# Table sets of ScalarE asked for by name in a linear attention, and silu of two gate units one product later

## The chip, the cores and the metric

The kernel runs on one core of one Trainium2 chip. The metric is the device time of one execution in microseconds (us). The engines are TensorE (PE; its weight loads are shown apart as PEld), VectorE (DVE), ScalarE (ACT), GpSimd (POOL) and SyncE (SP, which here issues most DMAs). ACT evaluates functions from a table that holds one set of functions at a time. An ACT_TABLE_LOAD brings in another set.

## The reference

One layer of a streaming encoder, 512 tokens of width 2048, all in float32. The part that matters here is the input projection and the gated linear attention behind it:

```python
proj = h @ w_in[i]
q_a, k_a, v_a, q_g, k_g, v_g, r_g, gate_lr = split_cols(proj, IN_SPLITS)
gate_logit = gate_lr @ w_gla_gate_up[i] + b_gla_gate[i]
log_a = jax.nn.log_sigmoid(gate_logit) / GLA_GATE_TAU      # 4 heads of 128 keys
o_g = gated_linear_attention(q_g, k_g, v_g, log_a)         # exp(b), exp(-b), exp(b_last - b), b a sum over a chunk
o_g = rms_norm(o_g, gla_norm_w[i])
y_g = o_g * jax.nn.silu(r_g)
x = x + jnp.concatenate([y_a, y_g], axis=-1) @ w_out[i]
```

Before it stands an RMSNorm, beside it a banded softmax attention (16 heads), and after it a gated MLP with a causal convolution and GELU, an embedding gate with a sigmoid, and a last RMSNorm.

## The kernel before, in words

Every large product is cut into units of 256 output rows by 512 tokens. A unit is computed by seven half-size products (P1, P2, P6, P5, P7, P3, P4 in this order) instead of eight. Each float32 operand is split into a high and a low part of float32r, so a product is three runs of 8 matmuls: high weights with high input, high weights with low input, low weights with high input. A product takes 2.72 us on PE.

One list, `steps`, holds all products of the program in order, and the loop at line 1350 emits one step after the other. What a step emits stays in program order on each engine: ACT, DVE and PE instructions go through the wrapper at line 64, which is why nearly every row of the profile bears L64. For a step i the loop emits in this order: the items of the agenda with key 0 (DMAs), the high half of the weights of step i+2 (`prep_high`, ACT, rows wsplit<-l and wsplit<-s), the items with key 1, the low half (`prep_low`, DVE, rows wsplit<-l,wsplit), the matmuls, the items with keys over 1, and last the eviction of the product's PSUM bank (`collect`). A product whose quarter of the output is new is copied out by ACT (rows u<-accA, u<-accC); another is added by DVE. The next product on the same bank waits for that. Split weights live in a ring of three pages, outputs of units in a ring of two, u0 and u1, in this part. So a unit's first copy waits until the unit before last has been stored.

The first stage, `linear` (line 1068), has ten units in this order: head 0, two value units, head 1, two value units, head 2, gate unit 0, gate unit 1, head 3. The stage after it, `front`, starts with the softmax heads. A head unit gives the keys and queries of a linear-attention head (`gla_head`). Its own ACT work is spread over the steps around it:

- two steps into the unit, `softplus` and `logs`: Abs (row e<-pz), Exp and Ln (rows e<-e), which give log_sigmoid together with DVE's lf, then DVE's running sum cs and the differences dd
- `powers` and `falls`, two steps later: four Exp (rows eb, en, dd, dec)
- during the units behind it, `root` and `rooted`: Identity (nwa), Ln and Exp (both rows rg) and Square (nwt) of the head's mean square; DVE finishes (rows nwt, rg) and scales the output (row og)

A gate unit (`after_gates`) multiplies its output by the norm of the input on DVE (u<-u,rb), applies Silu on ACT (u<-u), multiplies by the head's output on DVE (u<-u,on) and stores the operands of the output projection through SP (rows mix_R<-u, mix_N<-tp and so on).

The kernel does not say which table set ACT is to hold. When the program is built, an ACT_TABLE_LOAD is put ahead of each function that the set in force lacks, and the set is chosen per function: one for Exp, one for Ln, one for Silu.

Of the kernel before, what the change touches and what calls it, by code (L numbers as in the profile page):

```python
# [11 lines left out]
AF = mybir.ActivationFunctionType  # L12
# [31 lines left out]
def encoder_block(ctx: ExitStack, tc: tile.TileContext, A, out):  # L44
    nc = tc.nc
# [24 lines left out]
    vec, act, ten = InOrder(nc.vector), InOrder(nc.scalar), InOrder(nc.tensor)  # L70
# [13 lines left out]
    rb = cp.tile([P, T], F32, name="rb")  # L84
    rtok = cp.tile([P, TT], F32, name="rtok")
    cw = cp.tile([P, 2 * FB, 4], F32, name="cw")

    counts = {}

# [173 lines left out]
    def store_pair(xd, k, a, b, t=None):  # L263

        t = (page("x", "tp") if t is None else t).rearrange("p (o t) -> p o t", o=4)
        a0, a1, b0, b1 = a[:, 0:256], a[:, 256:512], b[:, 0:256], b[:, 256:512]
        ops = dict(R11=a0, R21=b0, R22=b1, N1=t[:, 0, :], T3=t[:, 1, :], N2=t[:, 2, :], T4=t[:, 3, :])

        def store(*names):
            for op in names if xd else ():  # L270
                store_operand(xd, op, k, ops[op])

        store("R11", "R21", "R22")
        vec.tensor_tensor(ops["N1"], a0, a1, ALU.subtract)
        store("N1")
        vec.tensor_tensor(ops["T3"], b1, a1, ALU.subtract)
        store("T3")
        vec.scalar_tensor_tensor(ops["N2"], ops["N1"], -1.0, b1, ALU.mult, ALU.subtract)
        store("N2")
        vec.scalar_tensor_tensor(ops["T4"], ops["N2"], -1.0, b0, ALU.mult, ALU.subtract)  # L280
        store("T4")
        return ops
# [573 lines left out]
    def after_gates(unit):  # L856
        g, M = unit.u - 8, unit.M

        def times():
            vec.tensor_tensor(unit.o, unit.o, M["on"], ALU.mult)  # L860

        def pair():
            ops = store_pair(mixd if g < 3 else None, 3 + g, unit.o[:, 0, :], unit.o[:, 1, :])
            if g == 3:
                tails[1] = ops

        return [(0, 1, lambda: vec.tensor_tensor(unit.o, unit.o, rb2, ALU.mult)),
                (0, 2, lambda: act.activation(unit.o, unit.o, AF.Silu))] + (
                    [(4, 1, times), (5, 1, pair)] if g < 2 else [(1, 1, times), (1, 3, pair)] if g == 2 else
                    [(0, 3, times), (0, 4, pair)])  # L870

# [2 lines left out]
    def gt(name, tag, cols=T):  # L874
        return gla["pool"].tile([P, cols], F32, tag=tag, name=name)
# [17 lines left out]
    def gla_head(unit):  # L893
# [14 lines left out]
            act.activation(e, e, AF.Exp, scale=-1.0)  # L908

        def logs():  # L910
            act.activation(M["e"], M["e"], AF.Ln, bias=1.0)

        def least():
# [9 lines left out]
                              ALU.subtract)  # L923

        def powers():
            for n, k in (("eb", 1.0), ("en", -1.0)):
                M[n] = gt(n, n)
                act.activation(M[n], M["cs"], AF.Exp, scale=k / TAU)
# [11 lines left out]
        def gates_begin():  # L940
            i = base[unit]
            for t, k, f in ((0, 0, load_v), (0, 6, logits), (1, 2, softplus), (1, 3, least), (2, 2, logs), (3, 1, sums),
                            (4, 1, powers), (4, 3, falls), (6, 1, decays)):
                agenda[i + t].append((k, f))
# [405 lines left out]
    for i, (unit, prod) in enumerate(steps[:-4]):  # L1350
# [19 lines left out]
        if i - len(steps) in EARLY:  # L1370
            p, op, g = EARLY[i - len(steps)]
# [160 lines left out]
```

## Time and profile before

| what | value |
|---|---|
| median of 3 runs (lowest to highest) | 2251.08 us (2249.51 to 2252.3) |
| the profiled execution | 2249.89 us |
| its span on the core | 2248.2 us |
| PE busy | 2196.9 us, 98% of the span |
| DVE busy | 1926.6 us, 86% |
| ACT busy | 1351.5 us, 60% |
| ACT_TABLE_LOAD | 31 in the ordered part and one at the start, 1283 ns each |
| mean granted clock of PE | 0.995 |

A busy PE is not a PE at its peak: ends of matmuls are modelled. What can be read well is where PE waits. A row of the timeline has start, duration, engine, line, operation, output <- input, shapes and count. In brackets stands the idle time of the engine before it and whose work ended that time.

### The profile page before, as it was taken

The numbers are of one execution on the slowest core, as the hardware profiler recorded it, in microseconds if no ns is written. First come the engines' busy times: TensorE is split into PE (matmuls) and PEld (weight loads), VectorE is DVE, ScalarE is ACT, GpSimd is POOL, SyncE is SP. The second block draws the span as 40 slices with busy tenths as digits, with TensorE's granted clock in tenths as the row PEclk, the third lists the DMA queues.
The fourth block names the chain that finished last, engine by engine and source line by source line (L and its number), as shares of the span: only waits on it lengthen the run. The fifth ranks groups of instructions, "written<-read, shape, count | busy, mean of one in ns | idle before, by whom it ended". The sixth has DMA issues, their size and how long they took to land. (4 is left out here: it accounts for less than half of the span.)

```text
span 2248.2 us, 46272 instructions
## 1 busy us (share of the span) xinstructions
PE 2196.9 (98%) x18588; PEld 2145.7 (95%) x18588; DVE 1926.6 (86%) x2636; ACT 1351.5 (60%) x2010; POOL 158.7 (7%) x196
## 2 busy tenths in 40 slices
PE   9999999999999999999999999999999999999995
PEld 8899989999889999999999999999999999999995
DVE  8476777999879888999988898889898887999996
ACT  9455565777665665555555555555564554667655
POOL 0000000000000100000000000010000100000000
PEclk9999999999999999999999999999999999999998
DMA  7476865667878987888888888888876968879993
GB/s 236 137 182 194 220 191 154 185 185 195 285 249 271 325 236 203 221 231 212 223 215 223 216 221 217 220 217 223 253 237 233 315 222 273 291 256 330 275 305 144
DMA packets 190760, 518.31 MB, mean 231 GB/s; under 512 B 20272, under 2 KB 66608, under 8 KB 190544
## 3 DMA queue, kind: packets, MB, share of 16 engines
q1 hardware_dynamic: 160272, 415.72, 54.4%
q0 software_dynamic: 25920, 93.33, 23.2%
q10 hardware_dynamic: 4352, 6.29, 0.8%
q8 instruction: 146, 2.39, 0.4%
q14 instruction: 70, 0.57, 0.1%
HBM read 441.86 MB, written 71.30 MB: 228 GB/s over the span
## 5 line engine op out<-in xcount | busy, mean ns | idle before, releaser
L64 DVE TENSOR_TENSOR wsplit<-l,wsplit 128x1024 fp32r<-128x1024 f32 (+1 forms) x478 | 573.0, 1200 | 116.9 <-ACT wsplit L64 115.9
L64 ACT ACTIVATE wsplit<-l 128x1024 fp32r<-128x1024 f32 (+1 forms) x478 | 497.7, 1042 | 290.7 <-PE accC L64 122.5
L64 DVE TENSOR_TENSOR wsplit<-s,wsplit 128x1024 fp32r<-128x1024 f32 (+1 forms) x251 | 300.9, 1200 | 68.6 <-ACT wsplit L64 68.0
L64 ACT ACTIVATE wsplit<-s 128x1024 fp32r<-128x1024 f32 (+1 forms) x251 | 260.7, 1039 | 61.0 <-PE accB L64 35.8
L64 ACT ACTIVATE u<-accA 128x256 f32<-128x256 f32 x302 | 114.1, 378 | 269.4 <-PE accA L64 266.3
L64 PE MATMUL accA<-up_T,wsplit 128*128 128x256 f32 x2112 | 253.6, 276 | 0.4 <-ACT wsplit L64 0.4
L64 PEld LDWEIGHTS accA<-up_T,wsplit 128*128 128x128 f32 x2112 | 245.8, 188 | 0.7 <-ACT wsplit L64 0.6
L64 DVE SCALAR_TENSOR_TENSOR cv<-u,cw,cv 128x511 f32<-128x511 f32 (+1 forms) x176 | 131.5, 747 | 3.1
L405 POOL DMA_DIRECT2D s<-in_w_up x88 | 76.3, 867 | 761.8 <-DMA s<-in_w_up 348.5
L64 PE MATMUL accA<-up_N,wsplit 128*128 128x256 f32 x1056 | 127.1, 276 | 1.3 <-DVE wsplit L64 1.3
L64 PE MATMUL accA<-dn_T,wsplit 128*128 128x256 f32 x1056 | 126.2, 276 | 1.9 <-DVE wsplit L64 1.7
L64 PE MATMUL accC<-up_N,wsplit 128*128 128x256 f32 x1056 | 126.8, 276 | 0.9 <-DVE wsplit L64 0.9
L64 PE MATMUL accB<-up_R,wsplit 128*128 128x256 f32 x1056 | 126.8, 276 | 0.6 <-DVE wsplit L64 0.6
L64 PE MATMUL accA<-up_R,wsplit 128*128 128x256 f32 x1056 | 126.9, 276 | 0.0
L64 PE MATMUL accC<-up_R,wsplit 128*128 128x256 f32 x1056 | 126.5, 276 | 0.0
L64 PEld LDWEIGHTS accA<-dn_T,wsplit 128*128 128x128 f32 x1056 | 122.6, 188 | 2.5 <-DVE wsplit L64 2.1
L64 PEld LDWEIGHTS accA<-up_N,wsplit 128*128 128x128 f32 x1056 | 123.0, 188 | 1.7 <-DVE wsplit L64 1.7
L64 PEld LDWEIGHTS accC<-up_N,wsplit 128*128 128x128 f32 x1056 | 122.9, 188 | 1.1 <-DVE wsplit L64 1.1
L64 PEld LDWEIGHTS accB<-up_R,wsplit 128*128 128x128 f32 x1056 | 122.9, 188 | 0.8 <-DVE wsplit L64 0.8
L64 PEld LDWEIGHTS accA<-up_R,wsplit 128*128 128x128 f32 x1056 | 122.9, 188 | 0.5 <-issue 0.5
L64 PEld LDWEIGHTS accC<-up_R,wsplit 128*128 128x128 f32 x1056 | 122.8, 188 | 0.0
L64 DVE TENSOR_TENSOR l<-l,l 128x1024 f32<-128x1024 f32 (+1 forms) x86 | 102.5, 1192 | 0.0
(338 smaller groups left out, 4227.4 us busy)
## 6 DMA issues: line engine op xcount, KB each, us to landing
l<-in_w_up SPq DMA_DIRECT2D x132, 512.0 KB, 4.6
s<-in_w_up SPq DMA_DIRECT2D x88, 512.0 KB, 5.0
s<-in_w_up POOLq DMA_DIRECT2D x88, 512.0 KB, 6.3
l<-in_w_dn SPq DMA_DIRECT2D x56, 448.0 KB, 5.3
l<-in_w_blk SPq DMA_DIRECT2D x48, 512.0 KB, 4.8
s<-in_w_blk SPq DMA_DIRECT2D x32, 512.0 KB, 4.4
s<-in_w_blk POOLq DMA_DIRECT2D x32, 512.0 KB, 7.6
l<-in_w_out SPq DMA_DIRECT2D x28, 512.0 KB, 4.5
```

The costliest lines, as they stand in the source:

```text
L64: ins = f(*args, **kw)
L405: nc.gpsimd.dma_start(t, src("L22" if name == "S1" else "L11"), accum_op=ALU.add)
```

## The change

The kernel gets a helper, `table(name)`, which asks for a table set by name at a place in ACT's order. `logs` asks for the set natural_log ahead of its Ln. `powers` asks for natural_log_exp_and_others, a set with Ln as well as Exp, ahead of its four Exp. And in the first two gate units Silu moves from the step behind the unit's last product, key 2, to the step after that, key 1.5.

```diff
+    def table(name):
+        tc.keep_in_program_order(nc.scalar.preload_act_table_set(name))
...
         return [(0, 1, lambda: vec.tensor_tensor(unit.o, unit.o, rb2, ALU.mult)),
-                (0, 2, lambda: act.activation(unit.o, unit.o, AF.Silu))] + (
+                (1 if g < 2 else 0, 1.5, lambda: act.activation(unit.o, unit.o, AF.Silu))] + (
                     [(4, 1, times), (5, 1, pair)] if g < 2 else [(1, 1, times), (1, 3, pair)] if g == 2 else
                     [(0, 3, times), (0, 4, pair)])
...
         def logs():
+            table("natural_log")
             act.activation(M["e"], M["e"], AF.Ln, bias=1.0)
...
         def powers():
+            table("natural_log_exp_and_others")
             for n, k in (("eb", 1.0), ("en", -1.0)):
```

Only ACT's list of instructions differs. DVE, PE, POOL and SP have the same instructions in the same order. ACT has 23 table loads where it had 32.

The first place is on ACT, while gate unit 1 begins: the root of head 2 (nwa, rg, rg, nwt) and Silu of gate unit 0 (u<-u 128x1024). Before:

```order
L64 ACTIVATE nwa<-msw,cols 128x512
L64 ACT_TABLE_LOAD
L64 ACTIVATE rg<-msw,cols 128x512
L64 ACT_TABLE_LOAD
L64 ACTIVATE u<-u 128x1024
L64 ACTIVATE u<-accA 128x256
L64 ACTIVATE wsplit<-s_2872 128x1024
L64 ACT_TABLE_LOAD
L64 ACTIVATE rg<-rg 128x512
L64 ACTIVATE nwt<-rg 128x512
L64 ACTIVATE wsplit<-s_2911 128x1024
```

and now:

```order
L64 ACTIVATE nwa<-msw,cols 128x512
L64 ACTIVATE rg<-msw,cols 128x512
L64 ACTIVATE u<-accA 128x256
L64 ACTIVATE wsplit<-s_2878 128x1024
L64 ACTIVATE rg<-rg 128x512
L64 ACTIVATE nwt<-rg 128x512
L64 ACT_TABLE_LOAD
L64 ACTIVATE u<-u 128x1024
L64 ACTIVATE wsplit<-s_2917 128x1024
```

The two loads around Ln and Exp of the root are gone, and Silu with its own load stands behind the root, not inside it.

The second place is on ACT, while head 3 begins: Silu of gate unit 1, the first copy out of head 3 (u<-accA), then Abs, Exp and Ln of its softplus. Before:

```order
L64 ACT_TABLE_LOAD
L64 ACTIVATE u<-u 128x1024
L64 ACTIVATE u<-accA 128x256
L64 ACTIVATE wsplit<-s_3153 128x1024
L64 ACTIVATE e<-pz,cols 128x512
L64 ACT_TABLE_LOAD
L64 ACTIVATE e<-e 128x512
L64 ACTIVATE wsplit<-s_3185 128x1024
L64 ACT_TABLE_LOAD
L64 ACTIVATE e<-e 128x512
L64 ACTIVATE u<-accA 128x256
```

and now:

```order
L64 ACTIVATE u<-accA 128x256
L64 ACTIVATE wsplit<-s_3158 128x1024
L64 ACTIVATE u<-u 128x1024
L64 ACTIVATE e<-pz,cols 128x512
L64 ACT_TABLE_LOAD
L64 ACTIVATE e<-e 128x512
L64 ACTIVATE wsplit<-s_3191 128x1024
L89 ACT_TABLE_LOAD
L64 ACTIVATE e<-e 128x512
L64 ACTIVATE u<-accA 128x256
```

Silu has lost its load and now stands between the copy and the softplus.

The third place is on ACT in the second softmax unit: the root of head 3. Before:

```order
L64 ACTIVATE nwa<-msw,cols 128x512
L64 ACT_TABLE_LOAD
L64 ACTIVATE rg<-msw,cols 128x512
L64 ACTIVATE u<-accA 128x256
L64 ACTIVATE wsplit<-s_3681 128x1024
L64 ACT_TABLE_LOAD
L64 ACTIVATE rg<-rg 128x512
L64 ACTIVATE nwt<-rg 128x512
```

and now:

```order
L64 ACTIVATE nwa<-msw,cols 128x512
L64 ACTIVATE rg<-msw,cols 128x512
L64 ACTIVATE u<-accA 128x256
L64 ACTIVATE wsplit<-s_3689 128x1024
L64 ACTIVATE rg<-rg 128x512
L64 ACTIVATE nwt<-rg 128x512
```

Two loads are gone and nothing has changed places. In the roots of heads 0 and 1, further ahead, two loads each are gone in the same way.

## The prediction

> **What bounds the kernel now.** I read the busy line of the page first, then the groups of ACT, then the busy time by stretches, and last the timeline of PE for its waits.
>
> ```profile
> span 2248.2 us, 46272 instructions
> PE 2196.9 (98%) x18588; PEld 2145.7 (95%) x18588; DVE 1926.6 (86%) x2636; ACT 1351.5 (60%) x2010; POOL 158.7 (7%) x196
> L64 ACT ACT_TABLE_LOAD x31 | 39.8, 1283 | 3.5 <-DVE cv L64 2.0 <-DVE x L64 0.6 <-ACT pp_o L64 0.4
> 150.00:200.00 50.00, 50.00 (x414) 48.05 (x412) 35.76 (x43) 32.26 (x42) 4.33 (x5) 1.00 0.77 207
> 200.00:250.00 50.00, 50.00 (x413) 48.28 (x413) 32.03 (x39) 28.18 (x38) 2.59 (x3) 1.00 0.71 203
> ```
>
> PE sets the time. A table load is worth something only where PE waits behind it. Nine loads go: 9 x 1.28 = 11.5 us of ACT's time, and this is not the gain. Four of them, in the roots of heads 0 and 1, fall between 150 and 250 us. There PE is busy 50.00 of 50.00 us twice (the first number after the length), while ACT works 32.26 and 28.18 us. They cost nothing now, hidden by PE's own matmuls, and ACT has over 17 us of idle time in each stretch before they could cost anything.
>
> The other five stand between 289 and 366 us. These are all waits of PE over 0.3 us from 285 to 600 us:
>
> ```profile
> 293.70 3.00 PE L64 MATMUL accA<-in_N,wsplit 128*128 128x256 f32 x24 [0.32 <-ACT u L64]
> 302.64 1.22 PE L64 MATMUL accA<-in_T,wsplit 128*128 128x256 f32 x8 [1.41 <-DVE wsplit L64]
> 317.40 3.00 PE L64 MATMUL accA<-in_N,wsplit 128*128 128x256 f32 x24 [1.28 <-ACT u L64]
> 324.03 3.00 PE L64 MATMUL accA<-in_T,wsplit 128*128 128x256 f32 x24 [0.91 <-ACT u L64]
> 330.30 2.97 PE L64 MATMUL accA<-in_T,wsplit 128*128 128x256 f32 x24 [0.55 <-ACT wsplit L64]
> 339.25 0.46 PE L64 MATMUL pat<-eb,en 128*128 128x128 f32 x2 [0.53 <-DVE eb L64]
> 373.31 2.99 PE L64 MATMUL accA<-in_T,wsplit 128*128 128x256 f32 x24 [0.79 <-ACT u L64]
> 379.44 1.21 PE L64 MATMUL accC<-in_R,wsplit 128*128 128x256 f32 x8 [1.33 <-DVE wsplit L64]
> ```
>
> They add up to 7.12 us. No more than this can be won here, and each has to be followed to what made it late.
>
> **First place, head 2's root and Silu of gate unit 0.** ACT and DVE:
>
> ```profile
> 287.36 3.30 PE L64 MATMUL accA<-in_R,wsplit 128*128 128x256 f32 x24
> 289.02 1.28 ACT L64 ACT_TABLE_LOAD   x1
> 290.32 0.69 ACT L64 ACTIVATE rg<-msw,cols 128x512 f32<-128x512 f32 x1
> 293.29 0.36 ACT L64 ACTIVATE u<-accA 128x256 f32<-128x256 f32 x1
> 293.55 1.05 ACT L64 ACTIVATE wsplit<-s 128x1024 fp32r<-128x1024 f32 x1
> 295.91 0.63 ACT L64 ACTIVATE rg<-rg 128x512 f32<-128x512 f32 x1
> 296.58 0.63 ACT L64 ACTIVATE nwt<-rg 128x512 f32<-128x512 f32 x1
> 297.24 0.69 DVE L64 SCALAR_TENSOR_TENSOR nwt<-nwt,nwa 128x512 f32<-128x512 f32 x1 [1.38 <-ACT nwt L64]
> 301.37 1.22 DVE L64 TENSOR_TENSOR wsplit<-s,wsplit 128x1024 fp32r<-128x1024 f32 x1
> 303.64 1.21 DVE L64 TENSOR_TENSOR u<-u,on 128x1024 f32<-128x1024 f32 x1
> ```
>
> From the load at 289.02 to the next function at 290.32 pass 1.30 us; that is the price of one load in a full queue. Without the loads and with Silu moved, Ln runs at 289.0 to 289.7 and the copy u<-accA can start when its product ends, 287.36 + 3.30 = 290.7, not 293.29. PE's wait of 0.32 goes. The weights follow at 290.95, the root's Exp one operation later at 291.9, Square at 292.6 (0.67 after Exp, as in the rows), ending 293.2. DVE's nwt starts at 293.3 instead of 297.24, 3.9 us earlier, and all that DVE does behind it moves by as much: the low half at 301.37 comes at 297.4 and is ready at 298.6. PE, now 0.32 earlier, needs it at 302.64 - 1.41 - 0.32 = 300.9. So the wait of 1.41 goes too. Silu with its one load runs from 293.2 to 295.5 and puts off the high half of these weights, but only to 296.5, before DVE gets to their low half; DVE's own use of Silu is u<-u,on at about 299.7. **Gain so far 0.32 + 1.41 = 1.73 us.**
>
> **Second place, Silu of gate unit 1 inside head 3's softplus.**
>
> ```profile
> 306.40 2.33 SPq L261 DMA_DIRECT2D mix_R<-u  x3
> DMA to landing us min/median/max: 8.6/9.6/9.8
> 312.86 1.06 ACT L64 ACTIVATE u<-u 128x1024 f32<-128x1024 f32 x1
> 316.96 0.39 ACT L64 ACTIVATE u<-accA 128x256 f32<-128x256 f32 x1 [3.05 <-DMA mix_R<-u]
> 323.08 0.63 ACT L64 ACTIVATE e<-e 128x512 f32<-128x512 f32 x1
> 323.61 0.37 ACT L64 ACTIVATE u<-accA 128x256 f32<-128x256 f32 x1
> 323.74 0.69 DVE L64 TENSOR_TENSOR lf<-lf,e 128x512 f32<-128x512 f32 x1 [0.71 <-ACT e L64]
> 323.70:339.20 15.50, 14.13 (x120) 13.77 (x120) 15.32 (x22) 10.66 (x17) 1.73 (x2) 1.00 0.83 222
> ```
>
> Here ACT waits 3.05 us for nothing of its own: the first copy of head 3 needs the page from which gate unit 0 is being stored. The stores go out at 306.40, behind DVE's u<-u,on and weight loads that DVE releases, and land some 9 us later at 316.9. DVE being 3.9 us earlier, issue and the burst of transfers ahead of it move alike, so I take 313.0 for the landing. PE would want its product at 317.40 - 1.28 - 1.73 = 314.4, so the wait of 1.28 goes.
>
> From there ACT is one unbroken chain: copy at 316.96, weights, Abs, Exp, weights, Ln, next copy at 323.61, 6.65 us. Silu is new in it; before, it ran at 312.86 in time that ACT then idled away. Its price is 1.06 less an overlap of 0.09, or 0.97, so 7.62. Next copy at 313.0 + 7.62 = 320.6, against 323.61: 3.0 us earlier. What waits behind Silu is this copy and Ln, and for Ln waits DVE (323.74), which from then to 339.2 is busy 15.32 of 15.50 us. So the product at 324.03, and the waits of 0.55 and 0.53 that hang on DVE's backlog, all move with Ln. **Gain up to 339 us: 3.0**, not 5.0, of which Silu takes back 0.97. The load that Silu loses at this place was in idle time: nothing.
>
> **Third place, head 3's root.**
>
> ```profile
> 361.06 3.30 PE L64 MATMUL accA<-in_R,wsplit 128*128 128x256 f32 x24
> 362.04 0.68 ACT L64 ACTIVATE nwa<-msw,cols 128x512 f32<-128x512 f32 x1
> 367.24 0.63 ACT L64 ACTIVATE rg<-rg 128x512 f32<-128x512 f32 x1
> 368.56 0.69 DVE L64 SCALAR_TENSOR_TENSOR nwt<-nwt,nwa 128x512 f32<-128x512 f32 x1 [1.39 <-ACT nwt L64]
> 372.90 0.36 ACT L64 ACTIVATE u<-accA 128x256 f32<-128x256 f32 x1
> 378.16 1.23 DVE L64 TENSOR_TENSOR wsplit<-s,wsplit 128x1024 fp32r<-128x1024 f32 x1
> ```
>
> Times of before. Ln follows nwa at 362.6, the copy comes when PE's product ends at 364.4, weights at 364.65, Exp at 365.6 instead of 367.24: 1.6 us, not 2 x 1.30, since the copy now has to wait for PE. DVE's nwt moves by 1.6, and the copy at 372.90 to 371.3, ahead of PE's need at 373.31 - 0.79 = 372.5: that wait goes. The low half at 378.16 moves to 376.6 and ends at 377.8. PE wants it at 379.44 - 1.33 - 0.79 = 377.3, so 0.5 of its wait stays. **Gain 0.79 + 0.8 = 1.6 us.**
>
> **Sum.** 3.0 + 1.6 = 4.6 us off the profiled execution of 2249.9: 2245.3. That execution is 1.2 us under the median of the runs, 2251.1, so I forecast 2246.5 for the median.
>
> **Bounds of what the trace does not show.** The landing of the stores: at the latest where it is now (316.96 stays, Silu costs 0.97, the third place gains 1.6: 0.6 in all); at the earliest, by the next unit's stores, which land 6.4 us after issue, at 308.8. Then the copy waits for PE alone, all six waits up to 339 go, 5.0, and the sum is 6.6.
>
> ```profile
> DMA to landing us min/median/max: 6.4/6.5/6.5
> L64 ACT ACTIVATE e<-e 128x512 f32<-128x512 f32 x8 | 5.1, 632 | 0.1
> ```
>
> I stay between, at 313.0, because the same burst as before goes ahead of the stores, only 3.9 us earlier. Exp and Ln from the combined set are not in the trace. From separate sets, four of each make the group above with a mean of 632 ns, and Exp of the root takes 0.63 as well. So I take no difference; twice 0.05 us on the chain at the third place would be the bound, a tenth of a microsecond either way.
>
> On the price of a switch, the Trainium skill ("ScalarE: Activation LUTs", section What ACT_TABLE_LOAD costs) gives 1283 ns for the load and about 1380 ns of drain, 2.66 us in all. The trace has the 1283, and the next function starts 0.02 us behind it, so no drain is seen. With it the nine loads would be an estimate of 24 us of ACT's time, but the waits of PE would still cap the gain at 7.1.
>
> **Rivals.**
>
> Stores land early (17%): the burst ahead of them thins out because its first load leaves sooner. For it speaks the 6.4 us of the next group; against it, that nothing is taken out of the burst. 2251.1 - 6 = about 2245.
>
> Stores do not move (12%): the queue and not the issue sets the landing, as 8.6 us or more here against 6.4 for the next group suggests. Then Silu in the chain eats part of the third place: 2250.5.
>
> The gain is given back later (8%). This row is the next wait of PE:
>
> ```profile
> 615.97 4.38 PE L64 MATMUL pp<-ps,wsplit 128*128 128x512 f32 x11 [2.91 <-ACT pp_o L64]
> ```
>
> If pp_o's stores were paced by the DMA queues and not by PE, an earlier PE would wait longer there: 2250 to 2251. Against it: the stores are issued behind PE's own products. And from 380 to 600 us no wait of PE over 0.3 us stands in the list, so nothing there can swallow time that PE has won.
>
> Slower (6%): loads released 4 us earlier slip ahead of the stores of gate unit 0 in the queue, which land later than now. From a landing 0.6 us later the third place's 1.6 is eaten (0.97 + 0.6). Each 512 KB ahead of them costs 2.4 us at the 222 GB/s of the row above; three of them make 316.96 into 324.0, Silu adds 0.97, and less the 1.6 some 6.4 us are lost: 2257.5. Against it: SP's order is unchanged.
>
> The change does not do what it says (3%): the program is loaded with its own switches as well. Then only the moved Silu counts, +1: 2252.
>
> **Chances.** Forecast 54%, early stores 17%, the others 12, 8, 6 and 3. About 0.2% (4.5 us) can be told from no change, and my 4.6 lies on that line: of the 54, 30 fall beyond it, which with 17 makes 47% faster. The remaining 24 with 12, 8, 3 and one of the 6 give 48% no change, and 5% slower. The range runs from the early stores to the unmoved ones, 2243.5 to 2250.5; the forecast's own is 2245 to 2248.
>
> **What would show it.** The profile of the changed kernel should have 22 loads in this group. PE's waits near 293, 302, 317 and 373 should be gone, those of 0.9, 0.55 and 0.53 still there, the last near 0.5. The copy of head 3 should still be released by mix_R, but some 4 us earlier, before PE wants its bank, with Silu behind it. DVE's nwt should come 3.9 and 1.6 us earlier against PE. A copy released no earlier, or by PE, makes my second step wrong; a longer wait at 616 us the assumption that nothing later takes time back.

## The result

| kernel | median of its runs | before, beside it | ratio, 95% interval |
|---|---|---|---|
| the change | 2245.74 us (15 runs) | 2250.80 us (15 runs) | 0.9979 (0.9972 to 0.9985) |

The change is 5.1 us faster by the medians, 4.7 by the ratio; 4.6 was forecast, and the time lies 0.8 us under the forecast of 2246.5. The profile that is read below is of an execution of 2245.14 us, against 2249.89 for the one before.

From the page, and from the view of groups, of the changed kernel:

```profile
span 2242.8 us, 46265 instructions
PE 2196.2 (98%) x18588; PEld 2145.4 (96%) x18588; DVE 1927.1 (86%) x2636; ACT 1339.5 (60%) x2001; POOL 158.7 (7%) x196
L64 ACT ACT_TABLE_LOAD x14 | 18.0, 1283 | 3.2 <-DVE cv L64 2.0 <-DVE x L64 0.6 <-ACT pp_o L64 0.4
L89 ACT ACT_TABLE_LOAD x8 | 10.3, 1283 | 0.1
```

ACT does 12.0 us less (1351.5 to 1339.5), the 22 loads of the ordered part are there (14 placed by the builder, 8 asked for at line 89), and the span is 5.4 us shorter. PE does the same work: 2196.2 us against 2196.9. So the time came out of PE's waits. Those over 0.3 us from 285 to 600 us were eight; now they are five (timeline of PE):

```profile
320.74 2.99 PE L64 MATMUL accA<-in_T,wsplit 128*128 128x256 f32 x24 [1.26 <-ACT u L64]
327.01 2.97 PE L64 MATMUL accA<-in_T,wsplit 128*128 128x256 f32 x24 [0.56 <-ACT wsplit L64]
335.96 0.46 PE L64 MATMUL pat<-eb,en 128*128 128x128 f32 x2 [0.54 <-DVE eb L64]
374.52 1.19 PE L64 MATMUL accC<-in_R,wsplit 128*128 128x256 f32 x8 [0.78 <-DVE wsplit L64]
383.32 1.25 PE L64 MATMUL ptr<-ident,sc 128*128 128x128 f32 x8 [0.48 <-DVE sc L64]
```

The waits near 293, 302, 317 and 373 are gone. The first three that are left are the 0.91, 0.55 and 0.53 of before, the fourth is what stays of 1.33, and the last is new. ACT at the three places, and DVE's nwt (of the first and the third) and lf:

```profile
291.06 0.39 ACT L64 ACTIVATE u<-accA 128x256 f32<-128x256 f32 x1 [1.10 <-PE accA L64]
293.60 1.28 ACT L64 ACT_TABLE_LOAD   x1
293.61 0.69 DVE L64 SCALAR_TENSOR_TENSOR nwt<-nwt,nwa 128x512 f32<-128x512 f32 x1
294.89 1.06 ACT L64 ACTIVATE u<-u 128x1024 f32<-128x1024 f32 x1
312.72 0.39 ACT L64 ACTIVATE u<-accA 128x256 f32<-128x256 f32 x1 [4.01 <-DMA mix_R<-u]
313.95 1.05 ACT L64 ACTIVATE u<-u 128x1024 f32<-128x1024 f32 x1
319.79 0.63 ACT L64 ACTIVATE e<-e 128x512 f32<-128x512 f32 x1
320.32 0.37 ACT L64 ACTIVATE u<-accA 128x256 f32<-128x256 f32 x1
320.45 0.69 DVE L64 TENSOR_TENSOR lf<-lf,e 128x512 f32<-128x512 f32 x1 [0.71 <-ACT e L64]
363.63 0.69 DVE L64 SCALAR_TENSOR_TENSOR nwt<-nwt,nwa 128x512 f32<-128x512 f32 x1
368.29 0.36 ACT L64 ACTIVATE u<-accA 128x256 f32<-128x256 f32 x1
```

At the first place the copy is released by PE, and Silu with its load stands behind the root. At the second the copy is still released by the stores, 4.2 us earlier than before, with Silu in the chain behind it: 7.60 us from copy to copy (312.72 to 320.32). DVE's nwt starts 3.63 us earlier at the first place (297.24 to 293.61), in an execution in which PE was 0.37 late, and 4.93 earlier at the third (368.56 to 363.63), where PE was 3.31 early: 4.0 and 1.6 against PE.

To see where PE gains, each of the 18588 matmuls of one trace was paired with the same one of another. The table gives how much later (+) or earlier (-) it starts than in the trace of before; the heads are times of the trace before. 285 us lies ahead of the three places. The loads taken from heads 0 and 1 lie ahead of it, where PE has no wait, so that column is the play of single executions. The names are those of the experiments below.

| kernel | 285 | 310 | 326 | 345 | 370 | 382 | 400 | 450 |
|---|---|---|---|---|---|---|---|---|
| the change | +0.37 | -2.08 | -3.30 | -3.31 | -3.31 | -4.95 | -4.07 | -4.31 |
| the change again | -0.17 | -2.62 | -1.42 | -2.97 | -2.97 | -4.60 | -4.37 | -4.31 |
| tables only | -0.03 | -1.42 | -1.37 | -1.36 | -1.36 | -2.97 | -2.60 | -2.84 |
| Silu only | +0.39 | -1.95 | +0.64 | -0.60 | -0.59 | -0.62 | -0.59 | -0.86 |
| gate unit 1 early | -0.37 | -2.82 | -4.16 | -4.18 | -4.18 | -5.81 | -5.95 | -6.19 |
| stores from N1 | +0.79 | -1.66 | -4.41 | -5.49 | -5.49 | -7.12 | -7.58 | -7.44 |
| heads 0, 1 back | +0.58 | -1.87 | -2.67 | -2.70 | -2.70 | -4.34 | -4.49 | -4.73 |
| three more loads | +0.23 | -2.22 | +3.05 | +3.06 | +3.07 | +1.46 | +1.26 | +1.03 |
| one set | +1.27 | -1.18 | -3.93 | -3.05 | -3.05 | -4.70 | -4.88 | -4.55 |
| load in idle time | -0.43 | -2.88 | -5.41 | -5.22 | -5.22 | -6.83 | -7.28 | -6.63 |
| the same again | +0.19 | -2.25 | -5.01 | -5.46 | -5.46 | -7.07 | -7.11 | -6.43 |
| head 3 back | -0.83 | -3.28 | -4.23 | -4.26 | -4.25 | -4.28 | -4.33 | -4.20 |
| the same again | +0.12 | -2.32 | -3.00 | -3.02 | -3.02 | -3.05 | -3.50 | -3.74 |

In the change, the first place gives 2.45 us (from +0.37 to -2.08), the second 1.23 more by 345, the third 1.64 between 370 and 382. The 2.45 is the same, 2.44 to 2.45, in all eleven traces that have both edits at the first place, wherever PE stood at 285. Behind 450 us the shift stays near -4.2 until 1650 us. From there on, and at 383 and 612, single executions differ by one to three microseconds, so totals are read from the timed runs.

### The profile page after: what moved, and what is told of

Its sections match the earlier page's. It is cut to its first block, busy times and chain, and to the rows that moved or that the text cites. A ratio compares the mean times of both kernels' runs of the same rounds, so it can differ in the third digit from the quotient of the medians.

```text
span 2242.8 us, 46265 instructions
## 1 busy us (share of the span) xinstructions
PE 2196.2 (98%) x18588; PEld 2145.4 (96%) x18588; DVE 1927.1 (86%) x2636; ACT 1339.5 (60%) x2001; POOL 158.7 (7%) x196
## 3 DMA queue, kind: packets, MB, share of 16 engines
q10 hardware_dynamic: 4352, 6.29, 0.8%
## 4 chain that ended last, share of the span: by engine, by line
PE 79%; DVE 10%; DMA 5%; ACT 4%; issue 2%; SPq 0%; ACTq 0%; DVEq 0%; POOLq 0%
PE accA L64 41%; PE accC L64 21%; PE accB L64 10%; DVE wsplit L64 3%; DMA l<-in_w_ple_gate 1%; DMA s<-in_w_v_a 1%; DVE u L64 1%; DVE l L64 1%; PE py L64 1%; PE ptr L64 1%; DMA ppd<-pp_o 1%; ACT wsplit L64 1%; PE psc L64 1%; PE v L243 1%; PE v L244 1%
```

## The experiments

The theory is the prediction's: a load or a Silu is worth what PE's wait behind it is worth, and at the second place ACT's chain counts from the landing of gate unit 0's stores. The rivals are that one of the two edits does it all, that a load costs its price wherever it stands, and that later work gives the gain back. Times in the text are differences of medians from before. The intervals reach some 2 us to each side, so smaller differences between two kernels are read from the traces.

### The two halves of the change

Tables only, both Silu back at their old place:

```diff
-                (1 if g < 2 else 0, 1.5, lambda: act.activation(unit.o, unit.o, AF.Silu))] + (
+                (0, 2, lambda: act.activation(unit.o, unit.o, AF.Silu))] + (
```

> The tables asked for by name, both Silu where they were. Theory (the two edits share the gain; the change is 4.7 us below the kernel before in its comparison): in head 2's root a load and Silu of gate unit 0 still stand between Ln and Exp, so ScalarE makes nwt about 2.3 us later than in the change (a load of 1.28 and a Silu of 0.97 ahead of it) and 1.3 to 1.6 earlier than before; the wait of 1.41 at 302.64 shrinks to 0.1 to 0.4, and TensorE stands 1.2 to 1.6 us earlier than before at 310. The stores of gate unit 0 land some 1.5 to 2 us later than in the change; Silu of gate unit 1 with its load lies in idle time, the chain behind the copy is 6.65 instead of 7.60, so the copy behind it comes about 1 us later than in the change. Head 3's root loses its loads as in the change (1.6). Total 2.8 to 3.8 us below before. Rival A (the tables do it all, the moved Silu nothing): 4.7 below before. Rival B (the moved Silu does it all): no change.

Measured: 2247.02 us against 2250.00, 0.9986 (0.9977 to 0.9996), 3.0 lower. PE at 310 is 1.39 us earlier than at 285, and its waits up to 325 us are these:

```profile
301.19 1.18 PE L64 MATMUL accA<-in_T,wsplit 128*128 128x256 f32 x8 [0.59 <-DVE wsplit L64]
316.04 3.00 PE L64 MATMUL accA<-in_N,wsplit 128*128 128x256 f32 x24 [1.34 <-ACT u L64]
322.68 2.99 PE L64 MATMUL accA<-in_T,wsplit 128*128 128x256 f32 x24 [0.92 <-ACT u L64]
```

The tables alone win the first wait, over half of the second (0.59 is left of 1.41), and the third place. The second place gives nothing: the copy behind the stores comes at 315.60, 2.9 us later than in the change where 1.5 to 2 was expected, and the wait near 316 is there as before. The chain behind it is 6.66 us, as expected.

Silu only, without the requests:

```diff
         def logs():
-            table("natural_log")
...
         def powers():
-            table("natural_log_exp_and_others")
```

> Both Silu moved as in the change, no table asked for by name, so a load stands ahead of every Ln and Exp of the roots. Theory: in head 2's root the copy of accA no longer has Silu and its load ahead of it, and nwt comes about 2.3 us earlier than before (load and Silu now behind it), but 1.3 to 2.6 later than in the change; the wait of 1.41 at 302.64 goes, TensorE stands 1.7 to 2.3 us earlier at 310. The stores of gate unit 0 land 1 to 2 us later than in the change and the chain behind the copy is 7.6 us as there. Head 3's root keeps both loads, so the waits of 0.79 and 1.33 near 373 to 380 stay: nothing gained there (the change has 1.6). Total 1.2 to 2.4 us below before. Rival A (the tables do it all): no change. Rival B (the moved Silu does it all): 4.7 below before.

Measured: 2248.70 us, 0.9995 (0.9985 to 1.0004), 1.3 lower. PE gains 2.34 us by 310, as expected, and nothing between 370 and 382, as expected. What was not expected is that against before it loses 2.6 us between 310 and 326 (1.2 of them are back by 345). Waits of PE, and busy time and granted clock by stretches (the clock is the third number from the end):

```profile
315.79 3.03 PE L64 MATMUL accA<-in_N,wsplit 128*128 128x256 f32 x24 [1.62 <-ACT u L64]
323.38 4.62 PE L64 MATMUL accA<-in_T,wsplit 128*128 128x256 f32 x24 [1.83 <-ACT u L64]
321.00:324.00 3.00, 1.17 (x10) 0.97 (x10) 2.11 (x3) 2.97 (x5) 0.29 (x1) 0.99 0.64 213
324.00:327.00 3.00, 3.00 (x16) 3.00 (x16) 2.97 (x4) 2.97 (x5) 1.43 (x2) 0.50 0.53 87
```

Behind the wait of 1.83 us PE runs at half its clock for 3.4 us: 24 matmuls take 4.62 us, not 2.99. So neither edit is worth 4.7 alone, though for the tables it is the trace that says so: by 382 us they have won 2.9 us and the change 5.3, while their interval reaches to 5.2. The medians of the halves add to 4.3, which the intervals do not tell from the whole. In the traces the halves have won 1.3 and 1.0 us by 345 and the change 3.7. Most of what is missing is the landing of single executions: the stores of gate unit 0 are issued 1.45 us earlier with the tables, 1.98 with Silu and 3.63 with both, which nearly adds, but they land 1.36, 1.61 and 4.24 earlier. Silu's 0.97 in the chain is paid in both kernels that have it there.

### What sets the second place

Silu of gate unit 1 alone back ahead of the copy:

```diff
-                (1 if g < 2 else 0, 1.5, lambda: act.activation(unit.o, unit.o, AF.Silu))] + (
+                (1 if g == 0 else 0, 1.5, lambda: act.activation(unit.o, unit.o, AF.Silu))] + (
```

> The change, with Silu of gate unit 1 alone put back ahead of the copy, where ScalarE stands idle 4.01 us for the stores of gate unit 0; it still needs no load there. Theory (the stores decide when the copy starts, and everything ScalarE has between that copy and the next is on TensorE's path): the chain from copy to copy goes from 7.60 to 6.6, TensorE's wait of 1.26 at 320.74 to about 0.3, and TensorE stands 0.9 to 1.1 us earlier at 325 and at 339. If nothing behind takes it back the total is 5.4 to 5.9 us below before (the change 4.7); if the weights of the wait at 383.32 (0.48, new in the change) land at a time of their own, that wait grows to 1.2 to 1.5 and the total stays 4.7. Rival (the place of this Silu is worth nothing, the waits of 1.26, 0.56 and 0.54 come from elsewhere): they stay as they are.

Measured: 2243.93 us, 0.9969 (0.9958 to 0.9980), 6.1 lower.

```profile
312.80 0.38 ACT L64 ACTIVATE u<-accA 128x256 f32<-128x256 f32 x1 [1.61 <-DMA mix_R<-u]
319.46 0.37 ACT L64 ACTIVATE u<-accA 128x256 f32<-128x256 f32 x1
319.88 2.99 PE L64 MATMUL accA<-in_T,wsplit 128*128 128x256 f32 x24 [0.93 <-ACT u L64]
```

The chain is 6.66 us, and PE at 345 is 0.87 us earlier than in the change. The wait stayed at 0.93, not 0.3, because PE was 0.74 us further ahead at 285 in this execution and the stores, issued 0.73 us earlier, took 0.81 longer to land. The wait at 383 is not there, so up to 600 us nothing was taken back. But then this profile, of the longest of the seven runs (2246.39 us), has a wait of 6.29 us near 612 where before has 2.91, and PE's lead falls from 6.2 us at 600 to 3.5 at 630.

The three stores of gate unit 0 read the quarter N1 of the page tp and follow DVE's N1 (`other` is set for g == 0). As many bytes leave at the same place of SP's queue, but they are N1's, so this kernel leaves three operands of the output projection out:

```diff
-        store("R11", "R21", "R22")
+        if not other:
+            store("R11", "R21", "R22")
         vec.tensor_tensor(ops["N1"], a0, a1, ALU.subtract)
+        for op in ("R11", "R21", "R22") if other else ():
+            store_operand(xd, op, k, ops["N1"])
```

> The change, but the three stores of the right operand of gate unit 0 read a quarter of the page that DVE writes at that moment instead of u; as many bytes leave at the same place of SP's queue, and mix_R holds other numbers there (wrong output). So u is free for the copy once DVE has read it, at about 304, and the copy waits for TensorE alone. Theory (the landing of these stores sets the start of the chain): the copy starts at 310 to 310.6 instead of 312.72, the next one at 317.7 to 318.3, the waits of 1.26 and 0.56 go, that of 0.54 at 335.96 shrinks below 0.3; TensorE stands 1.9 to 2.8 us earlier at 339 than in the change; total 6.2 to 7.2 us below before unless the wait at 383 grows by the same. Rival (the stores only happen to end then; TensorE or a weight transfer sets the copy): it starts at 312.7 as before, no change against the change.

Measured: 2243.58 us, 0.9967 (0.9954 to 0.9980), 6.4 lower.

```profile
310.53 0.38 ACT L64 ACTIVATE u<-accA 128x256 f32<-128x256 f32 x1 [0.39 <-PE accA L64]
318.13 0.36 ACT L64 ACTIVATE u<-accA 128x256 f32<-128x256 f32 x1
318.26 0.69 DVE L64 TENSOR_TENSOR lf<-lf,e 128x512 f32<-128x512 f32 x1 [0.72 <-ACT e L64]
333.76 0.46 PE L64 MATMUL pat<-eb,en 128*128 128x128 f32 x2 [0.26 <-DVE eb L64]
```

The copy is released by PE 2.2 us earlier, the chain behind it is 7.60 us again, the waits of 1.26 and 0.56 are gone. So the landing of the stores does set the start of the chain. And a second thing can be read: from DVE's lf to PE's first pat there are 15.50 us here, 15.51 in the change (320.45 to 335.96), 15.51 in before (323.74 to 339.25). It is so, within 0.01 us, in every trace in which PE is not slowed by its clock; behind a drop of 3.4 us it is 15.64. PE's place behind 336 us is DVE's lf plus 15.5, whatever the waits between.

### Loads where PE has no wait, and loads on its path

```diff
         def root():
+            if hd < 2:
+                table("natural_log")
...
         def rooted():
+            if hd < 2:
+                table("exp_and_others")
```

> The change, with the four loads of the roots of heads 0 and 1 put back (natural_log asked for ahead of their Ln, exp_and_others ahead of their Exp). Theory: TensorE has no wait between 150 and 285 us that they could lengthen, so four loads, 5.2 us of ScalarE, cost nothing: 4.3 to 5.2 us below before, as the change, and TensorE at 285 us where it is in before within 0.4. Rival (each load costs its 1.30 us wherever it stands): 5.2 us more than the change, no gain against before. It also shows the wait of 0.48 at 383.32 a second time: if it belongs to the change it is there again, if it is one execution's late weights (it is not in the three kernels with TensorE still further ahead nor in the one with it less far) it is not.

Measured: 2244.40 us against 2249.99, 0.9975 (0.9965 to 0.9985), 5.6 lower: four loads, 5.1 us of ACT, cost nothing. PE at 285 is 0.58 later than in before, where 0.4 was the bound expected, but kernels without these loads stand there from 0.83 earlier to 1.27 later. The wait at 383 is not there.

```diff
         def softplus():
+            for name in ("natural_log", "exp_and_others", "natural_log") if hd == 3 else ():
+                table(name)
```

> The change, with three loads more at one place: ahead of Abs in head 3's softplus (sets asked for in turn, none of them needed). Theory (the chain from the copy at 312.7 to the next is the path of TensorE there): it goes from 7.60 to 11.4 to 11.5 us, the wait of 1.26 at 320.74 to 5.1, those behind it stay, TensorE stands 3.8 to 3.9 us later at 339 than in the change, total 0.5 to 1.3 us below before. Rival A (a load also drains the queue, 2.66 us each in place of 1.30): 8.0 more than the change, 3.3 above before. Rival B (ScalarE's idle time takes them up): as the change.

Measured: 2249.70 us, 1.0001 (0.9992 to 1.0009), 0.3 lower, so 4 to 5 us above the change where 3.8 to 3.9 was expected; the intervals allow both. The chain is as expected, 11.59 us (313.32 to 324.91). The loads follow one another without a drain, three of them in 3.86 us. In the trace PE loses more than the chain, by its clock:

```profile
315.62 3.86 ACT L89 ACT_TABLE_LOAD   x3
325.33 5.49 PE L64 MATMUL accA<-in_T,wsplit 128*128 128x256 f32 x24 [5.86 <-ACT u L64]
325.00:328.00 3.00, 2.67 (x12) 2.67 (x13) 2.89 (x4) 2.98 (x6) 0.69 (x1) 0.50 1.01 233
328.00:331.00 3.00, 3.00 (x16) 3.00 (x15) 3.00 (x3) 2.62 (x6) 0.18 (x1) 0.50 0.92 152
```

The wait is 1.26 + 4.60, of which 3.99 are the longer chain and 0.60 a later landing (313.32 for 312.72), and behind it PE runs at half clock for 6 us: 5.49 us for 24 matmuls. DVE's lf comes 4.59 us later than in the change (325.04), and pat stands 17.38 behind it, not 15.51: 1.87 us are the clock's. Rival A, 2.66 us a load, is out by the row of the loads. The Trainium skill ("TensorE: Matmul & The Clock Gate", section Part 1: The HAM clock gate (the "warmup" mystery)) has the clock halved after at least one idle window of about 3.4 us, and restored after about as long a busy one. The wait of 5.86 agrees; the 1.83 of the kernel with Silu alone, and 1.86 below, do not, since no wait ahead of those drops was longer than 1.86.

### Better than the change

```diff
         def softplus():
+            if hd in (0, 3):
+                table("natural_log_exp_and_others")
...
         def logs():
-            table("natural_log")
...
         def powers():
-            table("natural_log_exp_and_others")
```

and Silu of gate unit 1 early as above.

> Silu of gate unit 1 ahead of the copy as in the run before, and in the linear attention one set for Exp and Ln, natural_log_exp_and_others, asked for ahead of Abs in heads 0 and 3 only: no load stands between Exp and Ln nor ahead of eb, eight loads fewer than the change, and one load is left in head 3's chain. Theory: the chain from copy to copy goes from 6.66 to 5.4 us, the waits of 0.93 at 319.88 and 0.56 at 326.15 go; DVE, which follows ScalarE's Ln with lf and then works without a gap, comes 1.3 earlier and no more, so the wait behind its eb near 334 is 0.4 to 0.9 and TensorE stands 1.2 to 1.5 earlier at 339 than with Silu moved alone; total 6.9 to 7.6 below before. In heads 1 and 2 the missing loads are worth nothing. Rival A (all three waits go, DVE has room): 7.8 to 8.2 below. Rival B (transfers behind take it back): 6.0 below, as the kernel with Silu moved alone.

Measured: 2242.47 us, 0.9968 (0.9958 to 0.9977), 7.5 lower. The interval overlaps that of the kernel with Silu of gate unit 1 early.

```profile
313.95 0.39 ACT L64 ACTIVATE u<-accA 128x256 f32<-128x256 f32 x1 [1.41 <-DMA mix_R<-u]
317.32 0.75 DVE L64 TENSOR_SCALAR lf<-pz,cols 128x512 f32<-128x512 f32 x1 [0.78 <-ACT e L64]
319.32 0.36 ACT L64 ACTIVATE u<-accA 128x256 f32<-128x256 f32 x1
327.14 2.96 PE L64 MATMUL accA<-in_T,wsplit 128*128 128x256 f32 x24 [1.32 <-DVE u L64]
```

The chain is 5.37 us, as expected, and the waits of 0.93 and 0.56 are gone. In their place PE waits 1.32 us for DVE's u, which was not expected. The load now stands ahead of Abs, and DVE waits 0.78 us for Abs ahead of lf<-pz,cols, where it had no wait before. So its lf<-lf,e comes 6.63 us behind the copy (at 320.58), against 6.79 with Silu moved alone: of the 1.29 us taken from ACT's chain, 0.16 reach DVE and PE. PE's shifts in the table show no more, since in this profile the copy starts 1.2 us later than in the change and PE was 1.27 us late at 285. The 1.4 us between the two medians are within the intervals, and this trace does not explain them.

```diff
         def softplus():
-            if hd in (0, 3):
+            if hd == 0:
                 table("natural_log_exp_and_others")
...
+        def silu():
+            act.activation(unit.o, unit.o, AF.Silu)
+            if g == 1:
+                table("natural_log_exp_and_others")
```

> As the kernel with one set, but the one load that was left in head 3's chain is asked for right behind Silu of gate unit 1, in ScalarE's idle time ahead of the copy. Theory: the chain goes to 4.1 us; ScalarE no longer holds TensorE there; DVE's lf comes 0.5 to 1.3 earlier (its split of the weights ahead of lf takes over as the limit), so the wait behind eb near 334 goes below 0.4 and the total falls 0.3 to 0.9 further, 7.4 to 8.2 below before. Rival (the copy's start at the landing of the stores is all that is left): as the kernel with one set.

Measured: 2243.20 us, 0.9968 (0.9956 to 0.9980), 6.8 lower, where 7.4 to 8.2 was expected.

```profile
311.33 1.28 ACT L89 ACT_TABLE_LOAD   x1
312.76 0.38 ACT L64 ACTIVATE u<-accA 128x256 f32<-128x256 f32 x1
316.70 0.37 ACT L64 ACTIVATE u<-accA 128x256 f32<-128x256 f32 x1
318.52 0.68 DVE L64 TENSOR_TENSOR lf<-lf,e 128x512 f32<-128x512 f32 x1
325.08 2.98 PE L64 MATMUL accA<-in_T,wsplit 128*128 128x256 f32 x24 [0.73 <-DVE u L64]
334.02 0.46 PE L64 MATMUL pat<-eb,en 128*128 128x128 f32 x2 [0.52 <-DVE eb L64]
```

The chain is 3.94 us. lf has no wait in brackets any more: DVE's own queue is the limit, PE waits for DVE's u, and pat stands 15.50 us behind lf as ever. So the last wait did not go below 0.4. The chain is 1.43 us shorter than in the kernel above, and lf stands 5.76 us behind the copy for 6.63: 0.87 of it reach DVE.

### The third place, and the two kernels side by side

The change with the loads put back in the root of head 3 alone (as above, `if hd == 3`), the change again, and the kernel with the load in idle time again, on one chip:

> The change, with the two loads of head 3's root alone put back (natural_log asked for ahead of its Ln, exp_and_others ahead of its Exp). Theory (place 3 is worth its two waits): the wait of 0.79 behind the copy of accA near 369 and that of 1.33 behind DVE's wsplit near 375 come back as in before, TensorE loses 1.5 to 1.8 us between 365 and 382 against the change and nothing elsewhere; total 2.9 to 3.5 us below before. Rival (a load costs 1.30 us and a later wait gives nothing back: both loads in full): 2.6 us lost, 2.1 below before. Rival (they lie in idle time as those of heads 0 and 1): as the change.

> The change itself, beside the kernel with the load in idle time on the same chip. Theory: 4.3 to 5.6 us below before; the wait of 0.48 near 383, which no later kernel showed, is one execution's late weights and is not in this profile, so TensorE stands 4.7 to 5.3 us (its offset at 285 us taken off) ahead of before at 400 us. Rival: the wait is the change's own and is there again.

> The kernel with one set for Exp and Ln, Silu of gate unit 1 ahead of the copy and the load right behind it, again, beside the change on the same chip. Theory: 1.5 to 2.5 us below the change (its place-2 waits of 1.26 and 0.56 gone, one of 0.7 behind DVE's u in their place), 6.5 to 7.5 below before. Rival (what is gained at 320 to 340 is lost again by 700): as the change.

| kernel | median | ratio, 95% interval |
|---|---|---|
| head 3 back | 2245.47 us | 0.9982 (0.9973 to 0.9991) |
| the change again | 2245.19 us | 0.9983 (0.9974 to 0.9992) |
| load in idle time again | 2242.11 us | 0.9969 (0.9958 to 0.9980) |

The kernel before beside them: 2250.31 us. The load in idle time is 3.1 us below the change beside it, more than the 1.5 to 2.5 expected, though the two intervals overlap, and 8.2 below before, where 6.5 to 7.5 was expected. In the traces PE is 2.1 to 2.3 us further ahead at 450 in its two executions than in the two of the change. With head 3's loads back, both waits of the third place are back:

```profile
369.06 2.99 PE L64 MATMUL accA<-in_T,wsplit 128*128 128x256 f32 x24 [0.79 <-ACT u L64]
375.19 1.18 PE L64 MATMUL accC<-in_R,wsplit 128*128 128x256 f32 x8 [1.33 <-DVE wsplit L64]
```

and PE gains 0.03 us between 370 and 382, against 1.61 to 1.65 in the ten traces without these loads. But the time was 4.8 us below before, not 2.9 to 3.5. It was timed once more.

> The kernel with the two loads of head 3's root put back, once more: its first timing was 4.84 us below before in the medians, where 2.9 to 3.5 was expected, though its trace has both waits of place 3 back. Theory (the waits are in the time and the first sample of 11 runs was a lucky one): 2.6 to 3.8 below. Rival (something later takes up what place 3 gains or loses): 4.4 to 5.4 below, as the change. In both, the waits of 0.79 near 369 and 1.33 near 375 are there, and TensorE gains nothing against before from 345 to 450 us, where the kernels without these loads gain 1.0 to 2.0.

Measured: 2246.44 us against 2249.80, 0.9986 (0.9977 to 0.9996), 3.4 lower; PE again gains 0.03 us at the third place. The two timings average 4.1 below before; the change, the change again and the change with heads 0 and 1 back, which has the same third place, average 5.3 (5.1, 5.1, 5.6). The difference of 1.2 is near the 1.64 of the traces, but these intervals cannot tell it from none: that the third place pays in full is shown by the traces up to 450 us and not by the timed runs.

The change again showed no wait near 383. It showed something else at 321:

```profile
321.01 4.63 PE L64 MATMUL accA<-in_T,wsplit 128*128 128x256 f32 x24 [1.86 <-ACT u L64]
321.00:324.00 3.00, 2.99 (x14) 2.99 (x15) 2.93 (x4) 2.98 (x4) 1.72 (x2) 0.52 0.52 108
```

The wait of 1.26 was 1.86 in this execution, the clock halved behind it, and the 24 matmuls there took 1.6 us longer. In four other executions with the same second place the wait was 1.26, 1.50, 1.67 and 1.80, and the clock held. So with Silu in the chain this place is at the edge of a drop. But little of such a drop stays: pat stands 15.64 behind lf for 15.51 (320.72 to 336.36), 0.13 us later, since PE would have waited for DVE there. PE at 400 is 4.2 us ahead with its offset at 285 taken off, where 4.7 to 5.3 was expected; PE stood 0.54 earlier at 285 than in the change's first trace, and the stores landed no sooner (the copy at 313.00 for 312.72).

## Why the prediction was right, step by step

**Heads 0 and 1: nothing.** Right: the four loads put back cost nothing (0.9975 against 0.9979 for the change).

**First place, 1.73.** The mechanism was right, the size too small: 2.45. The trace of the change ran 0.37 us late, so the copy at 291.06, forecast at 290.7, and the rest came as worked out. The term that was mis-sized is the price of a wait, which I took from the brackets. Rows of before:

```profile
290.50 2.88 PE L64 MATMUL accB<-in_R,wsplit 128*128 128x256 f32 x24
293.70 3.00 PE L64 MATMUL accA<-in_N,wsplit 128*128 128x256 f32 x24 [0.32 <-ACT u L64]
296.54 2.88 PE L64 MATMUL accC<-in_N,wsplit 128*128 128x256 f32 x24
```

Without a wait such rows start 2.72 us apart, their ends overlapping the next by 0.16. With the wait of 0.32 it is 3.20 and then 2.84: 0.60 more in all. By these rows a wait costs its bracket, the lost overlap of 0.16 and a slower start of 0.12. PE went from +0.37 to -0.24 where this wait was (0.61), and to -2.08 behind the second (1.84 for 1.41); where the wait of 0.79 was, at the third place, it gained 1.07.

**Second place, 3.0 up to 339.** The stores landed at 312.6 (313.0 forecast), the chain was 7.60 (7.62), the next copy 3.29 us earlier (3.0). The 0.91 grew to 1.26 since PE arrived earlier than I had it, by the mis-sized first place. That lf decides was right, and sharper than I wrote it: PE's shift at 345, 3.31, is lf's, 3.29 (323.74 to 320.45). That the landing moves with the issue held as well, with a scatter of a microsecond: from the first issue to the last landing it took 9.8 to 10.8 us in the twelve traces in which these stores hold the copy, and 10.5 in before. The lower end is the change's own trace:

```profile
302.77 1.59 SPq L264 DMA_DIRECT2D mix_R<-u  x3
DMA to landing us min/median/max: 8.8/8.9/9.2
```

and here is the one with Silu of gate unit 1 early, issued 0.73 us sooner and landing no sooner:

```profile
302.04 1.85 SPq L264 DMA_DIRECT2D mix_R<-u  x3
DMA to landing us min/median/max: 9.6/9.7/10.0
```

So 312.6 for 313.0 was partly luck of the one execution.

**Third place, 1.6.** Right: 1.64, the wait of 0.79 gone and 1.33 down to 0.78. I had 0.5 left: PE came 0.28 us sooner than I had it, by the price of the wait of 0.79, and waited that much longer for the same low half of DVE's. So here that price changed nothing.

**Sum, 4.6.** By the trace 5.3 up to 382, by the timed runs 4.7 to 5.1, with an interval from 3.4 to 6.3. The 0.7 that the trace has more is the price of a wait at the first place. For the same reason the 7.1 us of PE's waits were no bound of what can be won: with the stores from N1 PE has won 7.9 from 285 to 382, and a wait of 0.78 is left. In the change's first profile 0.9 was given back by 400, at a wait near 383 behind DVE, which itself had waited 1.24 us for weights (0.41 in before). No other of the kernels' profiles has that wait of PE, nor has the second profile of the change, so it is no part of the change.

**The rivals.** Early stores would have needed a copy at about 309; it came at 312.7. Unmoved stores would have had it at 317. The change gave nothing back at 612: the wait there is 2.92, as before 2.91. In other traces it is up to 6.29, but it does not grow with PE's lead: at 600 us PE is 1.0 late where it is 4.50, and 6.3 early where it is 3.05. What sets it was not followed up. No drain was seen, also with three loads in a row.

## What to carry to other kernels

Follow each wait of the bounding engine to what made it late, and price a cut there and nowhere else: the same 1.28 us load was worth 1.3 (each of the three more, by DVE's lf), nothing (heads 0 and 1), or, with the clock drop behind a longer wait, more than its length. Ask the builder for one table set that holds all functions of an alternating chain, and put the one load that is left, and any work that can go there, into time that the engine spends waiting for a transfer. And look at what the engine next in line does after the cut, and at what waits for the work behind the load's new place: here DVE took over after about 2 us of the 3.7 that ACT's chain could lose.

## What was not expected of the hardware

PE's granted clock fell to 0.50 behind waits of 1.83 and 1.86 us, and held behind 1.80 and 1.67 at the same place of the program; it stayed down for 3.41 us, and for 6.83 us from within a wait of 5.86. The clock's own records suggest what decides. In each of the fourteen traces the clock changes only at instants that lie a multiple of 3.41 us apart, and where these lie differs from execution to execution. So the time falls into stretches of 3.41 us, and both drops came at the end of a stretch that held the whole wait: 317.71 to 321.13 for the 1.86, 320.51 to 323.92 for the 1.83. The waits of 1.80 and 1.67 lay across the edge of two stretches, 0.95 and 0.85 us in one case, 1.24 and 0.43 in the other.

Take all stretches at full clock between 285 and 640 us of the fourteen traces, and add up PE's idle time in each. PE's ends are modelled, so these sums are not exact. All 12 stretches with more than 1.92 us of idle time were followed by half the clock, none with less than 1.83 was, and of the six between, four were. This is read from traces; no run moved a wait against the stretches to test it. What a drop costs is not the 1.6 us that 24 matmuls take longer, where PE would have waited behind them anyway: 0.13 us were left of it by pat.
